# A decoder layer on one core: where fillers, low parts and broadcasts are placed

## The chip, the core and the metric

The kernel runs on one core of one Trainium2 chip. The metric is the device time of one execution in microseconds (us). Five engines run their own instruction queues beside each other: TensorE (PE, with its weight loads, PEld), VectorE (DVE), ScalarE (ACT), GpSimd (POOL), and SyncE (SP), which here only issues DMA transfers.

## The reference

One layer of a hybrid decoder: 1024 tokens, width 1024, all float32. An RMSNorm, one wide input projection, three token mixers on its columns (gated DeltaNet, mLSTM, sparse attention), each with its own projection and gates, a sum, an output projection, a SwiGLU network and a gated per-layer embedding. Cut to the parts that the change touches:

```python
# A: gated DeltaNet, 4 heads, chunks of 64 tokens
decay = jnp.where(tril, jnp.exp(jnp.where(tril, diff, 0.0)), 0.0)      # diff = gc_i - gc_j
X = jnp.where(strict, einsum('nbhid,nbhjd->nbhij', kb, kc) * decay, 0)
T = lax.linalg.triangular_solve(eye + X, eye, lower=True, unit_diagonal=True)
u, w = T @ (vc * bc), T @ (kb * jnp.exp(gc)[..., None])
# B: mLSTM, 4 heads: decay matrices of the same kind from i and f gates
# C: sparse attention, 8 heads in 2 groups, head width 64, 128 queries at a time
o = g_cmp * o_compressed + g_sel * o_selected + g_win * o_window       # gates from u
# merge, FFN
y = sum_b sigmoid(gate_b) * (out_b @ w_b);  h = x + y @ w_out
h = h + (silu(n(h) @ w1) * (n(h) @ w3)) @ w2
h = h + sigmoid(n(h) @ w_gate) * (p @ w_proj)                           # the per-layer embedding
```

## The kernel before, in words

**Precision.** Operands of the large products are kept as pairs of fp32r tiles: a high part (a rounded copy, made by ScalarE) and a low part (what is left, a subtraction). A product is three fp32r passes: high by high, high by low, low by high. `split` makes such a pair.

**Weights.** `run_blocks` streams the weights in blocks of four 128x512 tiles. SP loads `wraw` (four buffers), ACT casts `whi` (L429), and POOL, or for some tiles DVE, subtracts `wlo` (L431). The blocks' matmuls are named `mm`. After every third inner step a block yields, and `advance(rate)` then lets generators at the side issue a step or more each, so that their small matmuls and vector work are woven between the block's matmuls. A side generator can call `pause(us)`: it then yields until so much woven time, counted as 1.4 us per advance, has gone by. It so sets how many of the blocks' matmuls are issued ahead of the generator's next matmul, and, since SP's loads are issued with the blocks, the order on SP too. Nothing else sets the order: each engine runs its queue as issued.

**Stages.** From the start to about 874 us the input projection runs with the mixers' preparation at the side: `gates_side`, then four `gdn_solve`, four `mls_side`, then the attention's keys and compression, and beside these `gdn_scan`, the recurrence. From 874 to about 1311 us `nsa_attend` (attention) is woven with blocks of the merge gates at a rate of 3.8. From 1311 us on come the three branch projections, the output projection, the FFN (whose weight and activation products use sums of quarters, `ffn_combine` building four sums T1 to T4 and their high and low parts for each of eight rows of the model), and the per-layer embedding.

**The solve of a GDN head.** `gdn_solve` computes the gram matrices (`gram`), transposes keys (`ktr`), writes the diagonal blocks to DRAM and reads them back in another layout (`zds`, `zb`), solves them on DVE with 15 short steps, sends the inverses through DRAM (`xds`, then `zd`), spreads them by L908 into `gW` and `gV`, pauses 14.0, and then multiplies them up level by level (`levq`, `levv`, `levw`, ...). `row_bcast` makes a row of decays stand in all 128 partitions: POOL multiplies the identity by the column (L747, `gcb_d`), and a matmul with a matrix of ones sums it, in fp32.

**Attention.** A task is a branch (window or selected), a query tile and a pair of heads. `att_scores` makes four score rows `S`, DVE and ACT turn them into P, and P is scaled by the inverse sum, which has been multiplied by the gate (L1476), at L1478. `att_values` walks the key blocks of the task before: transposes P (`ptr`), copies the result to `PT` (DVE at L1570, ACT at L1572), and one block later multiplies the values (`nso`), two products of 64 output rows each, one per group, which stand in different halves of the array. After each of four quarters of the scores, a quarter of the values steps is issued. The compressed values `cv` are two products of 64 rows too.

Of the kernel before, what the change touches and what calls it, by code (L numbers as in the profile page):

```python
# [38 lines left out]
COMBINE_LAG = 8.0  # L39
CMP_AT = 1, 3  # L40
# [19 lines left out]
def _constants():  # L60
# [44 lines left out]
    add("rowscale", np.where((m >= 4) & (m < 8), -1.0, 1.0))  # L105
# [30 lines left out]
def _blocks(w_in, w_branch, w_out, w_ffn_in, w_ffn_out, w_ple_gate, w_ple_proj):  # L136
# [7 lines left out]
    for dst, src, n in ((0, 2048, 4), (4, 4108, 4), (8, 2052, 4), (12, 4104, 4), (16, 5392, 24)):  # L144
        rows[:, dst:dst + n] = w_in[:, src:src + n]
# [81 lines left out]
class Trunk:  # L227
# [381 lines left out]
    def gates_block(self):  # L609
# [4 lines left out]
        def evac(ct, hf, ps):  # L614
            if hf == 0:
                self.tc.keep_in_program_order(
                    nc.vector.tensor_tensor(bias, self.chan["rowb"], self.rowscale, OP.mult))
            nc.scalar.activation(rows[:40, hf * 512:hf * 512 + 512], ps[:40], AF.Identity,
                                 bias=bias[:40], scale=self.rowscale[:40])
            if hf == 1:  # L620
                self.flags.add("rows")

        self.gaterows = rows
        return self.chan_block(self.u, evac, ncols=1)

    def gates_side(self):
# [3 lines left out]
        ps = self.ps("gtr")  # L630
        for tt in range(NT):
            self.tr(ps[:, tt * 40:tt * 40 + 40], self.gaterows[:40, tt * P:tt * P + P])
        gm = self.b2("gm")[:, :320].rearrange("p (t c) -> p t c", c=40)
        nc.scalar.activation(gm, ps[:, :320].rearrange("p (t c) -> p t c", c=40), AF.Copy)
# [39 lines left out]
        self.cum, self.gcol = cum, gcol  # L674
# [62 lines left out]
        self.ms, self.msc, self.msi, self.memt, self.mwks, self.mr = s, sc, si, emt, wks, r  # L737
# [3 lines left out]
    def row_bcast(self, col, name):  # L741
# [3 lines left out]
        for hf in range(2):  # L745
            d = self.b2(name + "_d")
            nc.gpsimd.tensor_tensor(d[:, :].rearrange("p (t c) -> p t c", c=P), bc(self.ident.unsqueeze(1), [P, 4, P]),  # L747
                                    bc(col[:, 4 * hf:4 * hf + 4].unsqueeze(2), [P, 4, P]), OP.mult)
            ps = self.ps(name)
            self.mm(ps, self.ones, d)  # L750
            out.append(ps)
# [46 lines left out]
    def gdn_solve(self, h):  # L798
# [10 lines left out]
        dps = self.row_bcast(self.cum[:, :, h], "gcb")  # L809
# [20 lines left out]
        for w in H:  # L830
            for hf in H:
# [8 lines left out]
                yield from self.pause(1.4)  # L840
# [69 lines left out]
        yield from self.pause(14.0)  # L910
# [136 lines left out]
    def mls_side(self, h):  # L1047
# [6 lines left out]
        dps = self.row_bcast(self.mr[:, :, h], "mrb")  # L1054
# [188 lines left out]
    def nsa_keys(self, n, i):  # L1243
# [9 lines left out]
        for hf in range(2):  # L1253
# [10 lines left out]
            yield from self.pause(3.0)  # L1264
# [10 lines left out]
    def nsa_compress(self):  # L1275
# [3 lines left out]
        cv = self.small("cv", [P, 64])  # L1279
# [3 lines left out]
        for i, n in enumerate("kv"):  # L1283
# [13 lines left out]
            dst = ckr if n == "k" else cv  # L1297
# [9 lines left out]
            for g in range(2):  # L1307
                nc.vector.tensor_copy(dst[64 * g:64 * g + 63], ps[64 * g:64 * g + 63, :64])
# [28 lines left out]
        self.dump("cv", cv)  # L1337
# [10 lines left out]
    def nsa_attend(self):  # L1348
# [12 lines left out]
        for t in tasks + [None]:  # L1361
            a = self.att_scores(*t) if t else iter(())
# [698 lines left out]
```

## Time and profile before

| | |
|---|---|
| median of 3 runs | 2394.88 us (2393.13 to 2399.14) |
| the profiled execution's own time | 2392.93 us |
| its span, first to last instruction | 2391.1 us, mean granted clock 0.987 |
| busy: PE, PEld | 96%, 77% of the span |
| busy: DVE, ACT, POOL | 56%, 36%, 33% |
| DMA | 183 MB, mean 77 GB/s |

How to read the views: a row of waits reads "engine, its work, its line <- engine and work that released it: total us, times, longest us". A row of the timeline is "start, us, engine, line, work, operands, shape, count", with the idle time just before and what ended it in brackets; neighbours overlap, since matmuls are pipelined. A row of windows gives a stretch's length and then the busy time (and instruction count) of PE, PEld, DVE, ACT, POOL, the granted TensorE clock, the DMA share and GB/s. The chain of waits gives start, length and what ran. A row of groups gives count, total busy us, mean ns of one, and the idle time before it. Matmuls carry the line of a helper (L242, transposes L248 or L250).

### The profile page before, as it was taken

The numbers are of one execution on the slowest core, as the hardware profiler recorded it, in microseconds if no ns is written. First come the engines' busy times: TensorE is split into PE (matmuls) and PEld (weight loads), VectorE is DVE, ScalarE is ACT, GpSimd is POOL, SyncE is SP. The second block draws the span as 40 slices with busy tenths as digits, with TensorE's granted clock in tenths as the row PEclk, the third lists the DMA queues.
The fourth block names the chain that finished last, engine by engine and source line by source line (L and its number), as shares of the span: only waits on it lengthen the run. The fifth ranks groups of instructions, "written<-read, shape, count | busy, mean of one in ns | idle before, by whom it ended". The sixth has DMA issues, their size and how long they took to land.

```text
span 2391.1 us, 34586 instructions
## 1 busy us (share of the span) xinstructions
PE 2286.2 (96%) x12840; PEld 1829.4 (77%) x12840; DVE 1338.2 (56%) x3088; ACT 856.3 (36%) x1832; POOL 782.9 (33%) x662
## 2 busy tenths in 40 slices
PE   8989898989999998999999999998999999999999
PEld 6777677878778996666665778986777777777789
DVE  5455555643223436888775446677555555555583
ACT  6424242423222334545454322452222222222362
POOL 2342424322122123322121151235444444444434
PEclk9999999999999999999999999999999999999999
DMA  6131212121122123111111643311111111111143
GB/s 230 50 96 40 92 40 65 59 64 45 63 77 80 45 93 107 58 54 45 50 45 50 228 164 129 128 57 36 53 49 54 49 49 51 51 53 53 53 133 128
DMA packets 121887, 183.05 MB, mean 77 GB/s; under 512 B 25275, under 2 KB 47204, under 8 KB 121720
## 3 DMA queue, kind: packets, MB, share of 16 engines
q1 hardware_dynamic: 121432, 180.72, 22.5%
q8 instruction: 101, 1.65, 0.3%
q14 instruction: 66, 0.54, 0.1%
q10 hardware_dynamic: 288, 0.14, 0.0%
HBM read 149.04 MB, written 31.76 MB: 76 GB/s over the span
## 4 chain that ended last, share of the span: by engine, by line
PE 77%; DVE 12%; issue 4%; POOL 3%; DMA 3%; ACT 2%; SPq 0%; POOLq 0%; ACTq 0%; DVEq 0%
PE mm L242 60%; PE nso L242 3%; PE ptr L250 2%; PE S L242 2%; POOL wlo L431 2%; DVE P L1478 1%; DVE zb L893 1%; DVE xb L894 1%; PE mops L242 1%; PE gks L242 1%; PE gpu L242 1%; ACT g_junk L838 1%; POOL alo L1796 1%; ACT whi L429 1%; PE levq L242 1%
## 5 line engine op out<-in xcount | busy, mean ns | idle before, releaser
L431 POOL TENSOR_TENSOR wlo<-wraw,whi 128x512 fp32r<-128x512 f32 x334 | 449.7, 1351 | 1063.9 <-ACT whi L429 818.9
L242 PE MATMUL mm<-u,whi 128*128 128x512 f32 x1888 | 632.7, 410 | 2.0 <-ACT mg L1606 2.0
L429 ACT ACTIVATE whi<-wraw 128x512 fp32r<-128x512 f32 x408 | 255.7, 630 | 470.2 <-PE mm L242 384.0
L242 PEld LDWEIGHTS mm<-u,whi 128*128 128x128 f32 x1888 | 341.4, 190 | 76.0 <-issue 11.5
L242 PE MATMUL mm<-u,wlo 128*128 128x512 f32 x944 | 379.2, 402 | 0.0
L242 PEld LDWEIGHTS mm<-u,wlo 128*128 128x128 f32 x944 | 178.3, 189 | 39.4 <-issue 1.2
L1839 DVE TENSOR_TENSOR fc<-fc,mm 128x512 f32<-128x512 f32 x140 | 95.3, 686 | 159.0 <-PE mm L242 158.9
L1880 DVE TENSOR_TENSOR h<-h,mm 128x512 f32<-128x512 f32 x176 | 118.6, 684 | 74.6 <-PE mm L242 72.1
L242 PE MATMUL mm<-whi,alo 128*128 128x512 f32 x352 | 141.6, 402 | 6.8 <-POOL alo L1796 6.8
L242 PE MATMUL mm<-whi,ahi 128*128 128x512 f32 x352 | 140.7, 400 | 5.5 <-ACT whi L429 5.5
L242 PE MATMUL mm<-wlo,ahi 128*128 128x512 f32 x352 | 140.6, 399 | 2.5 <-POOL wlo L431 2.5
L431 POOL TENSOR_TENSOR wlo<-ws,whi 128x512 fp32r<-128x512 f32 x60 | 84.3, 1405 | 148.7 <-ACT whi L429 148.7
L242 PE MATMUL mm<-u2hi,whi 128*128 128x512 f32 x304 | 121.1, 398 | 0.0
L242 PE MATMUL mm<-u2lo,whi 128*128 128x512 f32 x304 | 121.1, 398 | 0.0
L242 PE MATMUL mm<-u2hi,wlo 128*128 128x512 f32 x304 | 120.3, 396 | 0.0
L1472 ACT ACTIVATE P<-P,n_ng 128x640 f32<-128x640 f32 (+7 forms) x128 | 93.0, 728 | 64.1 <-DVE n_ng L1470 61.1
L429 ACT ACTIVATE whi<-ws 128x512 fp32r<-128x512 f32 x60 | 37.8, 630 | 174.9 <-DVE h L1880 130.4
L250 PE MATMUL ptr<-ident,P 128*128 128x128 f32 x528 | 89.8, 282 | 7.3 <-DVE P L1478 5.5
L250 PEld LDWEIGHTS ptr<-ident,P 128*128 128x128 f32 x528 | 59.6, 140 | 47.2 <-issue 28.3
L242 PE MATMUL mm<-whi,u 128*128 128x256 f32 x512 | 94.1, 283 | 0.1
L431 DVE TENSOR_TENSOR wlo<-wraw,whi 128x512 fp32r<-128x512 f32 x74 | 69.5, 939 | 35.5 <-ACT whi L429 35.4
L242 PEld LDWEIGHTS mm<-whi,alo 128*128 128x128 f32 x352 | 66.8, 190 | 27.2 <-POOL alo L1796 11.6
(497 smaller groups left out, 5048.9 us busy)
## 6 DMA issues: line engine op xcount, KB each, us to landing
wraw<-in_w_dram SPq DMA_DIRECT2D x408, 256.0 KB, 2.7
mgs<-mg SPq DMA_DIRECT2D x48, 256.0 KB, 2.3
mgld<-mgs SPq DMA_DIRECT2D x48, 256.0 KB, 5.6
xt<-in_x_dram SPq DMA_DIRECT2D x8, 512.0 KB, 4.8
xt<-in_x_dram SPq DMA_DIRECT2D x32, 128.0 KB, 3.7
sg<-pps SPq DMA_DIRECT2D x32, 128.0 KB, 3.5
out_dram<-sg SPq DMA_DIRECT2D x32, 128.0 KB, 2.8
pps<-ppst SPq DMA_DIRECT2D x8, 256.0 KB, 2.0
```

Source lines behind the costliest of these rows:

```text
L242: return self.nc.tensor.matmul(out, lhsT, rhs, start=start, stop=stop).ins
L250: self.nc.tensor.transpose(out, in_, self.ident[:n, :n])
L429: nc.scalar.activation(hi, t, AF.Copy)
L431: eng.tensor_tensor(lo, t, hi.bitcast(F32), OP.subtract)
L838: nc.scalar.activation(junk, ps[:, q * P:q * P + P], AF.Square, accum_out=ssq[:, w, 4 * hf + q:4 * hf + q + 1])
L893: nc.vector.tensor_tensor(tmp[:, :m, m:], bc(Z[:, :m, m:m + 1], shp), bc(X[:, m:m + 1, m:], shp), OP.mult)
L894: nc.vector.tensor_tensor(X[:, :m, m:], X[:, :m, m:], tmp[:, :m, m:], OP.subtract)
L1472: nc.scalar.activation(pts[i][:, :nk], pts[i][:, :nk], AF.Exp, bias=ng[:, i:i + 1], accum_out=sm[:, g, i % 2:i % 2 + 1])
L1478: nc.vector.tensor_scalar(pts[i][:, :nk], pts[i][:, :nk], sm[:, g, i % 2:i % 2 + 1], None, OP.mult)
L1796: nc.gpsimd.tensor_tensor(lo, t, hi.bitcast(F32), OP.subtract)
L1839: nc.vector.tensor_tensor(t, x, ps, OP.add)
L1880: nc.vector.tensor_tensor(self.h[tt][s], self.h[tt][s], ps, OP.add)
```

## The change

1. **Gates block.** The 40 gate columns stand twice in a 128-column weight tile, at 0 and at 64. Four small DVE casts put their low parts at 64 to 103, in place of the second copy. Each half of the tokens then needs two passes of eight matmuls (weights by high, weights by low) rather than three; 104 rows are kept, `gates_side` transposes rows 0 to 39 and 64 to 103, and DVE adds the two.
2. **Decays.** `row_bcast` takes a column as a high and a low part (`col_split`), multiplies the identity by each on POOL, and sums them by two fp32r matmuls where one fp32 matmul stood. Four GDN heads (`gcb`) and four mLSTM heads (`mrb`) call it, each for two halves.
3. **Pauses.** 14.0 becomes 24.0 ahead of the levels of `gdn_solve`; 1.4 becomes 3.0 behind its second `ktr`; 3.0 becomes 6.0 in `nsa_keys` for the first half.
4. **Attention.** `att_values` transposes two key blocks in one step and multiplies the two of the step before; its steps are issued after the second, third and fourth quarter of the scores. The queries' preparation, `att_query`, is issued one task ahead. `cv` becomes block diagonal, one product of 128 rows. The gate (L1476) becomes the second scalar of the scaling of P.
5. **Low parts and sums from POOL to DVE.** The low parts of T1 to T4; the activations' low parts `alo` for the first two rows and every other half; the last sum of the embedding.
6. **Branch inputs.** For the second and third branch the split of each loaded tile is issued later, by 9.0 us and 2.56 us more per tile of matmul time, rather than at once.

The diff, cut to its core:

```diff
     for dst, src, n in ((0, 2048, 4), (4, 4108, 4), ...):
-        rows[:, dst:dst + n] = w_in[:, src:src + n]
+        rows[:, dst:dst + n] = rows[:, 64 + dst:64 + dst + n] = w_in[:, src:src + n]
...
+        def gen(wb):
+            for wh, wl in wb:
+                k2 = lambda t: t[:, :].rearrange("p (k c) -> p k c", k=2)[:, :, 64:104]
+                nc.vector.tensor_copy(k2(wh), k2(wl).bitcast(F32))
+            for hf in range(2):
+                ps = self.ps("mm", "mm")
+                for kc in range(KC):
+                    uh, ul = self.u(kc, hf)
+                    w = wb[kc // 2][0][:, kc % 2 * 256:kc % 2 * 256 + P]
+                    self.mm(ps, w, uh, kc == 0, False)
+                    self.last_mm = self.mm(ps, w, ul, False, kc == KC - 1)
...
+    def col_split(self, name, x):
+        hi, lo = self.small(name + "hi", list(x.shape), F32R), self.small(name + "lo", list(x.shape), F32R)
+        nc.vector.tensor_copy(hi, x)
+        nc.vector.tensor_tensor(lo, x, hi.bitcast(F32), OP.subtract)
+        return hi, lo
...
-            d = self.b2(name + "_d")
-            nc.gpsimd.tensor_tensor(d..., bc(self.ident...), bc(col[:, 4 * hf:4 * hf + 4]...), OP.mult)
             ps = self.ps(name)
-            self.mm(ps, self.ones, d)
+            for i, col in enumerate(cols):
+                d = self.b2(name + "_d", F32R)
+                nc.gpsimd.tensor_tensor(d..., bc(self.ident...), bc(col[:, 4 * hf:4 * hf + 4]...), OP.mult)
+                self.mm(ps, self.ones_r, d, i == 0, i == 1)
...
-                yield from self.pause(1.4)
+                yield from self.pause(3.0 if w else 1.4)
...
-        yield from self.pause(14.0)
+        yield from self.pause(24.0)
...
-            yield from self.pause(3.0)
+            yield from self.pause(6.0 if hf == 0 else 3.0)
...
-            nb = prev["nb"] + 2 if prev else 0
+            nb = -(-prev["nb"] // 2) + 2 if prev else 0
...
-                upto = -(-nb * (i + 1) // 4)
+                upto = -(-nb * i // 3)
...
+                if after and after[0] == "w" and after[2] == 0:
+                    if i == 0:
+                        ahead = self.att_query(after[1])
+                        next(ahead)
+                    elif i == 3:
+                        next(ahead)
...
-                nc.vector.tensor_tensor(sm[:, g], sm[:, g], gate[:, g], OP.mult)
                 for i in (n - 1, n):
-                    nc.vector.tensor_scalar(pts[i][:, :nk], pts[i][:, :nk], sm[:, g, i % 2:i % 2 + 1], None, OP.mult)
+                    nc.vector.tensor_scalar(pts[i][:, :nk], pts[i][:, :nk], sm[:, g, i % 2:i % 2 + 1],
+                                            gate[:, g, i % 2:i % 2 + 1], OP.mult, OP.mult)
...
-        for kb in range(nb + 1):
-            if kb < nb:
+        for kb in range(0, nb + 2, 2):
+            new = []
+            for b in range(kb, min(kb + 2, nb)):
                 ...
-            if pend is not None:
-                b, pt_ = pend
+                new.append((b, pt))
+            for b, pt_ in pend:
                 for g in range(2):
                     ...
-            pend = (kb, pt) if kb < nb else None
+            pend = new
             yield
...
-            for g in range(2):
-                gp = slice(64 * g, 64 * g + 64)
-                self.mm(o[gp, cols], st["cv"][gp], ct[gp, :256], False, hp == 1)
+            self.mm(o[:, cols], st["cv"].rearrange("p g d -> p (g d)"), ct[:, :256], False, hp == 1)
...
                 if first:
                     self.tc.keep_in_program_order(dma)
-                hi, lo = self.l2("yhi", F32R), self.l2("ylo", F32R)
-                self.split(hi, lo, t, scale)
-                res[kk, hf] = (hi, lo)
+                    parts(kk, hf, t)
+                else:
+                    self.later(Y_LAG + 2.56 * (4 * hf + kk), lambda kk=kk, hf=hf, t=t: parts(kk, hf, t))
...
-            nc.gpsimd.tensor_tensor(lo, t, hi.bitcast(F32), OP.subtract)     # part(), T1 to T4
+            nc.vector.tensor_tensor(lo, t, hi.bitcast(F32), OP.subtract)
...
-            nc.gpsimd.tensor_tensor(lo, t, hi.bitcast(F32), OP.subtract)     # put(), alo
+            (nc.vector if f < 2 or f % 2 and hf == 0 else nc.gpsimd).tensor_tensor(lo, t, hi.bitcast(F32), OP.subtract)
...
-                nc.gpsimd.tensor_tensor(t, t, h, OP.add)                     # the embedding's last sum
+                nc.vector.tensor_tensor(t, t, h, OP.add)
```

Where a pause is woven with blocks, the tables of instructions show the move. On SP, in the solve of the first head, before: the way of the solve's small blocks through DRAM (`zds`, `zb`, `xds`, `zd`) between weight loads (`wraw`) and stores of the merge gates (`mgs`).

```order
L882 DMA zds<-zd 128x8x16
L415 DMA wraw<-in_w_dram 128x512
L1608 DMA mgs<-mg 128x512
L884 DMA zb<-zds 64x256
L415 DMA wraw<-in_w_dram 128x512
L1608 DMA mgs<-mg 128x512
L415 DMA wraw<-in_w_dram 128x512 x3
L898 DMA xds<-xb 64x2x256
L1608 DMA mgs<-mg 128x512
L415 DMA wraw<-in_w_dram 128x512
L901 DMA zd<-xds 128x8x16 x2
```

The same place on SP with the change:

```order
L920 DMA zds<-zd 128x8x16
L1656 DMA mgs<-mg 128x512
L922 DMA zb<-zds 64x256
L416 DMA wraw<-in_w_dram 128x512 x3
L1656 DMA mgs<-mg 128x512
L416 DMA wraw<-in_w_dram 128x512
L936 DMA xds<-xb 64x2x256
L1656 DMA mgs<-mg 128x512
L939 DMA zd<-xds 128x8x16 x2
```

The order of the four transfers is kept, one store still stands between `xds` and the two reads of `zd`, and no weight load stands there now. On PE the rows `mm` of 128x512 between a head's last gram and its first `levq` number 89, 89, 90 and 90 in the four heads before, and 132 in each with the change. The last rows of the first stage's side work (`ncmp`, `nctr`, `khtr`) stand 16 `mm` earlier in PE's order, which is what the gates block has lost.

On PE in the attention, at a window task (`nvw` are its values), before:

```order
L242 MATMUL mm<-u,whi 128x512
L242 MATMUL nso<-PT,nvw 64x256 x2
L250 MATMUL ptr<-ident,P 128x128 x4
L242 MATMUL nso<-PT,nvw 64x256 x2
L242 MATMUL S<-khh,qT 128x256
L242 MATMUL S<-kll,qT 128x256
L242 MATMUL mm<-u,whi 128x512
L242 MATMUL nso<-PT,nvw 64x256 x2
L250 MATMUL ptr<-ident,P 128x128 x4
```

With the change, at the like place:

```order
L243 MATMUL mm<-u,whi 128x512
L251 MATMUL ptr<-ident,P 128x128 x4
L243 MATMUL nso<-PT,nvw 64x256 x6
L243 MATMUL S<-khh,qT 128x256
L243 MATMUL S<-kll,qT 128x256
L251 MATMUL ptr<-ident,P 128x128 x4
L243 MATMUL S<-khh,qT 128x256
L243 MATMUL S<-kll,qT 128x256
```

In the whole program the 132 pairs of `nso` over window and selected blocks (one product of 64 rows for each group) stand in 126 unbroken runs before and in 85 with the change, where 14 pairs are split by other work between their two products. Of the blocks' `mm` 469 stand between the first `S` and the last `nso` before, and 380 with the change.

On DVE in `ffn_combine` (`uw` builds the sums T1 to T4, `sil` is the FFN's gate product), before:

```order
L1769 TENSOR_TENSOR uw<-u2hi,u2lo 128x512 x3
L1805 TENSOR_TENSOR sil<-sil,mm 128x512
L1774 TENSOR_TENSOR uw<-uw 128x512
L1776 TENSOR_TENSOR uw<-uw 128x512
L1778 TENSOR_TENSOR uw<-uw 128x512
L1769 TENSOR_TENSOR uw<-u2hi,u2lo 128x512
L1781 TENSOR_TENSOR uw<-uw 128x512
L1805 TENSOR_TENSOR sil<-sil,mm 128x512
```

With the change:

```order
L1825 TENSOR_TENSOR uw<-u2hi,u2lo 128x512 x3
L1830 TENSOR_TENSOR uw<-uw 128x512
L1832 TENSOR_TENSOR uw<-uw 128x512
L1820 TENSOR_TENSOR utT1l<-uw,utT1h 128x512
L1834 TENSOR_TENSOR uw<-uw 128x512
L1820 TENSOR_TENSOR utT3l<-uw,utT3h 128x512
L1825 TENSOR_TENSOR uw<-u2hi,u2lo 128x512
L1820 TENSOR_TENSOR utT2l<-uw,utT2h 128x512
L1837 TENSOR_TENSOR uw<-uw 128x512
L1862 TENSOR_TENSOR sil<-sil,mm 128x512
L1820 TENSOR_TENSOR utT4l<-uw,utT4h 128x512
L1853 TENSOR_TENSOR alo<-sil,ahi 128x512 x2
```

The four subtractions that make the low parts, and the first two `alo`, now stand in DVE's queue between the sums, where POOL ran them before.

More of the change, by code (lines that the diff above doesn't have):

```diff
@@ L39 @@
 COMBINE_LAG = 8.0
+Y_LAG = 9.0
 CMP_AT = 1, 3
@@ L617, in evac @@
                     nc.vector.tensor_tensor(bias, self.chan["rowb"], self.rowscale, OP.mult))
[L618 to L619 removed]
+            nc.scalar.activation(rows[:104, hf * 512:hf * 512 + 512], ps[:104], AF.Identity,
+                                 bias=bias[:104], scale=self.rowscale[:104])
             if hf == 1:
                 self.flags.add("rows")
+        def gen(wb):
[9 more added lines that the diff above has]
+                    self.last_mm = self.mm(ps, w, ul, False, kc == KC - 1)
+                    if kc % 3 == 2:
+                        yield
+                evac(0, hf, ps)
+                self.passed(KC * 0.43)
+                yield
         self.gaterows = rows
[L624 removed]
+        return gen
     def gates_side(self):
@@ L629, in gates_side @@
         yield from self.need("rows")
-        ps = self.ps("gtr")
-        for tt in range(NT):
-            self.tr(ps[:, tt * 40:tt * 40 + 40], self.gaterows[:40, tt * P:tt * P + P])
         gm = self.b2("gm")[:, :320].rearrange("p (t c) -> p t c", c=40)
-        nc.scalar.activation(gm, ps[:, :320].rearrange("p (t c) -> p t c", c=40), AF.Copy)
+        for r in (0, 64):
+            ps = self.ps("gtr")
+            for tt in range(NT):
+                self.nc.tensor.transpose(ps[:, tt * 40:tt * 40 + 40], self.gaterows[r:r + 40, tt * P:tt * P + P],
+                                         self.ident[r:r + 40, r:r + 40])
+            p3 = ps[:, :320].rearrange("p (t c) -> p t c", c=40)
+            if r == 0:
+                nc.scalar.activation(gm, p3, AF.Copy)
+            else:
+                nc.vector.tensor_tensor(gm, gm, p3, OP.add)
         yield
@@ L673, in gates_side @@
         nc.scalar.activation(ekd, p8[:, 4, :, 0:4], AF.Exp)
-        self.cum, self.gcol = cum, gcol
+        self.cumhl, self.gcol = self.col_split("cum", cum[:, :, 0:4]), gcol
+        self.ones_r = sm("ones_r", [P, P], F32R)
+        nc.vector.tensor_copy(self.ones_r, self.ones)
         yield
@@ L807, in gdn_solve @@
         half = lambda ap, hf: ap[:, hf * 512:hf * 512 + 512]
-        dps = self.row_bcast(self.cum[:, :, h], "gcb")
+        dps = self.row_bcast([c[:, :, h] for c in self.cumhl], "gcb")
         yield
@@ L1053, in mls_side @@
         yield from self.need("mls_gates", ("m", h, "k"))
-        dps = self.row_bcast(self.mr[:, :, h], "mrb")
+        dps = self.row_bcast([c[:, :, h] for c in self.mrhl], "mrb")
         yield
@@ L1307, in nsa_compress @@
             for g in range(2):
-                nc.vector.tensor_copy(dst[64 * g:64 * g + 63], ps[64 * g:64 * g + 63, :64])
+                rows = slice(64 * g, 64 * g + 63)
+                nc.vector.tensor_copy(ckr[rows] if n == "k" else cv[rows, g], ps[rows, :64])
             yield
@@ L1360, in nsa_attend @@
         prev = None
-        for t in tasks + [None]:
+        for _ in self.att_query(0):
+            pass
+        for n, t in enumerate(tasks + [None]):
             a = self.att_scores(*t) if t else iter(())
+            after = (tasks + [None] * 2)[n + 1]
             b = self.att_values(prev) if prev else iter(())
             cur = None
-            nb = prev["nb"] + 2 if prev else 0
+            nb = -(-prev["nb"] // 2) + 2 if prev else 0
             done = 0
@@ L1397, in att_query @@
             out.append(t)
-        return out
+        yield
     def att_scores(self, br, qt, hp):
@@ L1614, in load_y, with parts @@
         res = {}
+        def parts(kk, hf, t):
+            hi, lo = self.l2("yhi", F32R), self.l2("ylo", F32R)
+            self.split(hi, lo, t, scale)
+            res[kk, hf] = (hi, lo)
         for hf in range(2):
```

28 lines of the change are left out of this document (15 added, 13 removed).

## The prediction

> **What bounds the kernel now.** I read the page's busy shares first, then what TensorE (PE) waited for, then the stretches in which it waited.
>
> ```profile
> PE 2286.2 (96%) x12840; PEld 1829.4 (77%) x12840; DVE 1338.2 (56%) x3088; ACT 856.3 (36%) x1832; POOL 782.9 (33%) x662
> ```
>
> PE is the bound: 2391.1 − 2286.2 = 104.9 us of the span are idle, and everything else must come from work removed from PE or from a slower clock. The waits say what ended the idle time:
>
> ```profile
> PE levq L242 <- DVE gW L908: 30.0, 4, 8.5
> PE mm L242 <- POOL alo L1796: 6.8, 11, 1.7
> PE mm L242 <- POOL wlo L431: 6.2, 7, 2.5
> PE qtr L248 <- DVE qstk L1388: 6.2, 8, 1.7
> PE mm L242 <- ACT whi L429: 5.5, 1, 5.5
> PE ptr L250 <- DVE P L1478: 5.5, 12, 0.8
> PE khtr L248 <- ACT khht L1261: 3.2, 2, 1.7
> PE ktr L250 <- ACT g_junk L838: 3.0, 3, 1.3
> PE nso L242 <- DVE PT L1570: 3.0, 3, 1.5
> ```
>
> These nine make 69.4 of the 104.9 us, and the change aims at each of them. The first is four waits, one per GDN head. What it costs beyond the idle time is in the stretches:
>
> ```profile
> 160.00:170.00 10.00, 10.00 (x164) 8.00 (x162) 2.67 (x4) 1.22 (x2) 2.54 (x2) 0.78 0.11 34
> 960.00:1020.00 60.00, 56.24 (x306) 37.42 (x306) 50.87 (x199) 33.17 (x82) 17.90 (x18) 1.00 0.20 67
> 1020.00:1080.00 60.00, 56.73 (x324) 36.74 (x324) 52.79 (x199) 31.40 (x73) 15.86 (x16) 1.00 0.14 49
> 1630.00:1640.00 10.00, 6.11 (x16) 4.51 (x17) 7.16 (x8) 4.49 (x8) 10.00 (x7) 0.55 0.17 57
> ```
>
> After PE stood still the granted clock falls (0.78 in 160 to 170, 0.55 in 1630 to 1640), so such a wait costs its length and some us more. In the attention (the rows of 60 us) the clock is 1.00, PE is busy 56 to 57 of 60 and VectorE (DVE) already 51 to 53.
>
> **1. The pause ahead of levq: −37.**
>
> ```profile
> 158.25 1.27 DVE L908 TENSOR_TENSOR gW<-zd,c 128x512 f32<-128x512 f32 x1 [6.14 <-DMA zd<-xds]
> 159.67 1.97 PE L242 MATMUL levq<-gW,zak 64*64 64x64 f32 x32 [7.85 <-DVE gW L908]
> 167.05 1.15 PE L242 MATMUL levq<-gW,zak 64*64 64x64 f32 x32
> 1699.24 57.75 PE mm L242 x246
> ```
>
> PE waits 7.85 us for `gW`, which itself waited for the inverse to come back through DRAM. The chain's row of 246 `mm` in 57.75 us gives 0.235 us for one. The order puts 132 rather than 89 or 90 of them between the last gram and levq, 43 × 0.235 = 10.1 us of work, against 7.5 us of idle per head (30.0 / 4; the longest is 8.5). That leaves 1.6 to 2.6 us if `gW` is not later. I take it not to be: on SyncE the order of the four transfers is kept, with one store between `xds` and `zd` as before. The first levq took 1.97 us where the warm one took 1.15, and the `mm` around it run slow too; a clock of 0.78 over 10 us is 2.2 us lost, of which I count 1.7 per head, 7 in all. So −30 − 7 = −37. If `gW` comes 3 us later, 1 us per head stays and some of the slow clock: −26. No work is removed here, so the fillers must come from elsewhere. They are taken from the blocks behind, which go on to the mLSTM and attention preparation; in the order, the last items at the side stand where they stood in the stream of `mm`, 16 rows earlier, which is what the gates block lost. So the pause doesn't push work past the stage's end.
>
> **2. ktr and khtr: −4.3** of the 6.2 us in their two rows, by 1.6 and 3.0 more of woven time against longest waits of 1.3 and 1.7; −2 to −6.2.
>
> **3. Gates block: −3.1.** 16 matmuls fewer, 16 × 0.235 = 3.8; eight more transposes, which by the row below are 0.9 busy and about 0.7 on the path. DVE's four casts and one addition lie beside PE, which has the next block. −2 to −3.8.
>
> ```profile
> L250 PE MATMUL gtr<-ident,gaterows 40*128 40x40 f32 x8 | 0.9, 235 | 0.0
> 177.21 1.72 PE gcb L242 x4
> 173.14 1.04 POOL L747 TENSOR_TENSOR gcb_d<-ident,cum 128x512 f32<-128x512 f32 x1
> ```
>
> **4. Broadcasts: −6.2.** The two fp32 matmuls of a head are four records and 1.72 us on the chain; four fp32r ones are 4 × 0.235 = 0.94. Eight calls: 8 × 0.78 = 6.2. POOL does 16 more products of 1.04 us. It is busy 33% of the span, and I take them as hidden, with 1 us put into term 10; if nothing hid them, +16.
>
> **5. Attention, products: −9.**
>
> ```profile
> 961.63 0.65 PE L242 MATMUL nso<-PT,nvs 128*64 128x256 f32 x4
> 962.22 0.65 PE L242 MATMUL nso<-PT,cv 64*64 64x256 f32 x4
> 962.80 0.73 PE L242 MATMUL mm<-u,whi 128*128 128x512 f32 x2
> 1083.01 1.08 PE L242 MATMUL nso<-PT,nvw 128*64 128x256 f32 x8 [1.47 <-DVE PT L1570]
> 1084.02 0.66 PE L250 MATMUL ptr<-ident,P 128*128 128x128 f32 x4
> ```
>
> A pair of half-array products (four records) holds PE from 961.63 to 962.22, 0.59 us; two pairs from 1083.01 to 1084.02, 1.01 us. So a pair is 1.01 − 0.59 = 0.42 and leaving a run costs 0.17; entering costs something too, which no row isolates, and I estimate 0.1. Runs fall from 126 to 85: 41 × 0.28 = 11.5 saved. 14 pairs are broken, and I let each product then take 0.42 alone, 14 × 0.42 = 5.9 lost: −5.5. `cv` is 0.58 from 962.22 to 962.80; one product of 128 rows by 256 columns in fp32 is half of a 128x512 (1.72 / 2 = 0.86), 0.43, and it enters no other mode: 16 × 0.22 = −3.5. The ends: no gain from fewer runs and broken pairs at full price +6 less `cv`, +2; broken pairs free −16.
>
> **6. Attention, waits: −9.** The rows `qtr`, `ptr` and `nso` are 14.7 us. The query, one task ahead, should take its 6.2 whole. The rest waits for DVE, which loses the 64 gate products,
>
> ```profile
> L1476 DVE TENSOR_TENSOR n_sum<-n_sum,cgate 128x2 f32<-128x2 f32 x64 | 19.4, 304 | 0.7
> ```
>
> 19.4 us, but now finds its values in three quarters of a task rather than four. I take a third of the remaining 8.5: −9, from 0 to −15.
>
> **7. FFN sums: −11.**
>
> ```profile
> 1592.32 0.68 DVE L1776 TENSOR_TENSOR uw<-uw 128x512 f32<-128x512 f32 x1
> 1593.04 1.70 DVE L1778 TENSOR_TENSOR uw<-uw 128x512 f32<-128x512 f32 x1
> 1592.89 1.30 POOL L1764 TENSOR_TENSOR utT1l<-uw,utT1h 128x512 fp32r<-128x512 f32 x1 [17.80 <-ACT utT1h L1763]
> 1625.40 0.50 PE L242 MATMUL mm<-whi,alo 128*128 128x512 f32 x1 [1.72 <-POOL alo L1796]
> 1631.37 0.79 PE L242 MATMUL mm<-whi,ahi 128*128 128x512 f32 x1 [5.48 <-ACT whi L429]
> 1634.68 0.79 PE L242 MATMUL mm<-wlo,ahi 128*128 128x512 f32 x1 [2.52 <-POOL wlo L431]
> ```
>
> The same DVE subtraction took 0.68 us alone and 1.70 when POOL ran beside it, and POOL's own took 1.30 to 1.76. So each low part on POOL slowed both. On DVE alone a set of T1 to T4 with its low parts and two `alo` is 12 operations of about 0.65, 8 us, within the 8.0 us of matmul time that the kernel's lag sets between two of them, though with nothing to spare. POOL is then free for `wlo`, and the three waits, 9.7 us with 2 more of slow clock behind (0.55 in 1630 to 1640), should go nearly whole: −11. If DVE falls behind at that rate half comes back: −5.
>
> **8. alo in the later rows: −4.7.**
>
> ```profile
> 1822.07 0.63 ACT L1795 ACTIVATE ahi<-fc 128x512 fp32r<-128x512 f32 x1 [1.95 <-DVE fc L1857]
> 1822.78 1.28 POOL L1796 TENSOR_TENSOR alo<-fc,ahi 128x512 fp32r<-128x512 f32 x1 [1.29 <-ACT ahi L1795]
> 1824.12 0.51 PE L242 MATMUL mm<-whi,alo 128*128 128x512 f32 x1 [0.52 <-POOL alo L1796]
> ```
>
> About 0.5 us ten times (6.8 less the 1.7 already counted): a DVE subtraction of 0.68 ends 0.6 sooner than POOL's 1.28. −4.7, from 0 to −5.1.
>
> **9. Tail and branch inputs: −4.** Near the end POOL does two sums between weights' low parts, and PE waits for the second:
>
> ```profile
> 2315.71 2.06 POOL sg L1967 x2
> 2317.78 1.68 POOL wlo L431
> 2319.50 2.54 PE mm L242 x19
> 1348.95 0.50 PE L242 MATMUL mm<-yhi,whi 128*128 128x512 f32 x1 [1.24 <-DVE acc L1658]
> ```
>
> 2.06 of POOL go, so PE starts up to 1.8 sooner; the branch loads' splits no longer stand before `acc`, 1.24 and a like one; and a little at the very end. −1 to −4.5.
>
> **10. New waits: +6.** Nothing in the trace shows them. A stretch with fewer fillers behind the solve, attention with 380 `mm` rather than 469, the POOL products: 0 to +25, the upper end being the attention's waits once over (14.7) and, for the first stage, one head's wait for `gW` and those before khtr (7.5 + 3.2). I take the lower part, since PE's idle time outside the named waits is only 104.9 − 69.4 = 35.5 us in the whole program.
>
> **The sum.** −37 − 4.3 − 3.1 − 6.2 − 9 − 9 − 11 − 4.7 − 4 + 6 = −82.3. On the profiled execution's 2392.93 that is 2310.6; the median of the runs is 1.95 above the profiled one, so 2312.6, and I say 2312.
>
> **Rivals.**
>
> *The pause only moves the wait.* If the return through DRAM is tied to the blocks' loads, `gW` comes later with the pause, and about half of term 1 stays: 2312 + 19 = 2331. For it: `gW` waited for the transfer, not for DVE. Against: the order of the queue.
>
> *Attention becomes VectorE's.* DVE is at 51 to 53 of 60 us. With 89 fewer `mm` as cover (21 us of PE work, moved into the time after it), DVE has to do its work in less time. If its busy share can't pass 90%, terms 5 and 6 give nothing and some 5 us come on top: 2312 + 18 + 5 = 2335. Against: 19.4 us of its work go.
>
> *No new waits at all, and every term near its far end:* 2312 − 6 − 16 = 2290.
>
> [...]
>
> [...]
>
> **How the numbers follow.** Forecast 0.57, the pause rival 0.12, DVE 0.16, all lands 0.12, half clock 0.03. The likeliest's own range is 2290 to 2330. With the DVE rival and a little over it the range is 2288 to 2345, and what lies outside is part of the all-lands case and the half clock, and misses of several terms at once. A change within 0.3% (7 us, about what a measurement of this kernel tells from none) needs 75 us of the sum to fail: 0.02. Slower is the half clock at its price: 0.03. Faster 0.95.
>
> **What would show it.** Idle before levq under 1 us and the clock at 1.00 in the 20 us after; `nso` runs of eight records or more, at 0.42 per pair; no `qtr` wait; DVE below 55 of 60 in the attention; no wait over 1 us between 1620 and 1640's counterpart; `gcb` at 0.94. The forecast is wrong if PE's waits on DVE in the attention exceed 15 us, if the time before levq merely shifts to `gW` again, or if the granted clock falls there.

## The result, and the profile after

The change takes 2328.11 us (median; 2327.02 to 2329.65), against 2394.01 us for the kernel before on the same chip: a ratio of 0.9721, 95% interval [0.9704, 0.9738]. The forecast was 2312, the range 2288 to 2345. So 66 us were gained where 82 were expected; the study asks where the other 16 went. The profiled execution took 2327.02 us, its span is 2325.2.

The page's busy times of the change:

```profile
PE 2263.7 (97%) x12800; PEld 1836.2 (79%) x12800; DVE 1332.0 (57%) x3096; ACT 852.3 (37%) x1832; POOL 729.1 (31%) x616
```

PE's idle time fell from 104.9 to 61.5 us, its busy time by 22.5 us. The waits on PE in the change (the longest groups, others left out):

```profile
PE ptr L251 <- DVE P L1525: 7.5, 12, 1.1
PE gytr L251 <- DVE vtok L1050: 5.4, 2, 3.1
PE warm L251 <- DMA ident<-in_c_dram: 5.0, 1, 5.0
PE u2tr L251 <- DVE u2lo L321: 4.7, 3, 2.0
...
PE mm L243 <- POOL wlo L432: 4.1, 5, 3.1
PE mtr L251 <- DVE m_tmp L737: 2.9, 1, 2.9
...
PE mm L243 <- ACT utT4h L1819: 2.0, 1, 2.0
PE gpu L243 <- DVE gvn L1025: 1.9, 3, 0.9
...
PE gks L243 <- DVE gS L1032: 1.5, 2, 1.0
PE khtr L249 <- ACT khht L1299: 1.5, 2, 0.8
```

The rows before levq, qtr and for `alo` are gone. In their place stand `gytr` (the transposes at the end of a GDN head's recurrence), a wait of 3.1 us for `wlo`, and a longer one for `m_tmp` (ahead of `mtr`, a transpose among the mLSTM gates), none of which the kernel before had at this size. `gpu` and `gks` are small products of the recurrence. The first levq in the timeline of the change, and stretches around it, around gytr and in the attention (windows):

```profile
171.45 1.15 PE L243 MATMUL levq<-gW,zak 64*64 64x64 f32 x32
```

```profile
160.00:170.00 10.00, 6.92 (x24) 5.41 (x24) 1.43 (x1) 0.60 (x1) 3.96 (x3) 0.83 0.51 142
170.00:180.00 10.00, 10.00 (x180) 7.88 (x179) 2.67 (x4) 0.60 (x1) 1.05 (x1) 1.00 0.01 2
228.00:238.00 10.00, 6.91 (x30) 5.37 (x29) 5.92 (x10) 4.09 (x20) 2.44 (x3) 0.83 0.36 132
926.00:986.00 60.00, 56.58 (x311) 39.80 (x312) 52.07 (x202) 33.84 (x84) 19.35 (x19) 0.97 0.17 58
986.00:1046.00 60.00, 57.72 (x351) 41.24 (x346) 51.91 (x205) 34.32 (x78) 13.62 (x13) 1.00 0.14 49
```

levq no longer waits and is warm (1.15 us), but just ahead of it, in 160 to 170, PE is busy for only 6.92 of 10 us, and again around gytr.

By stages, from the first start of a stage's first matmul in the two timelines: up to the first `S` the change is 33.7 us earlier (921.3 to 887.6); from there to the first branch product it gains another 12.7 (to 1333.6 and 1287.2, both including the 89 `mm` that moved behind the attention); to the first product with `ahi` 1.5; to the last one 15.2; to the end 2.8. So the FFN gave what was forecast, the attention a third less, and the first stage 33.7 where the terms 1 to 4 made 50.6.

The two traces let a stage be split further, into PE's idle time, what slow clock cost (by an estimate half of PE's busy time wherever the clock record stands at a half: from one `mm` to the next it is 0.427 us there in the median, and 0.231 at full clock, in both traces), and the rest, which is PE's work. Up to the first `S` idle time fell from 53.9 to 33.7 us, the cost of slow clock from 14.1 to 8.5, and the work from 853.3 to 845.5. From there to the first branch product idle time fell from 19.0 to 12.2, slow clock went from none to 1.7, and the work fell from 393.2 to 385.7. Stages are used below where the whole time, in which stretches of half clock come and go from one execution to the next (the mean granted clock was 0.992 to 0.994 in the four runs of the change), is too coarse; each is read from one profiled execution of a kernel.

### The profile page after: what moved, and what is told of

Same layout as the page of the kernel before. It is cut to its first block, busy times and chain, and to the rows that moved or that the text cites. A ratio compares the mean times of both kernels' runs of the same rounds, so it can differ in the third digit from the quotient of the medians.

```text
span 2325.2 us, 34431 instructions
## 1 busy us (share of the span) xinstructions
PE 2263.7 (97%) x12800; PEld 1836.2 (79%) x12800; DVE 1332.0 (57%) x3096; ACT 852.3 (37%) x1832; POOL 729.1 (31%) x616
## 4 chain that ended last, share of the span: by engine, by line
PE 84%; DVE 10%; issue 2%; ACT 2%; DMA 1%; POOL 1%; SPq 0%; ACTq 0%; POOLq 0%; DVEq 0%
PE mm L243 68%; PE nso L243 3%; PE ptr L251 2%; PE S L243 2%; DVE P L1525 1%; PE mops L243 1%; PE gks L243 1%; PE gram L243 1%; PE gpu L243 1%; DVE P L1514 1%; POOL wlo L432 0%; DVE uw L1825 0%; DVE kT L824 0%; DVE xn L1778 0%; PE u2tr L251 0%
## 5 line engine op out<-in xcount | busy, mean ns | idle before, releaser
L432 POOL TENSOR_TENSOR wlo<-wraw,whi 128x512 fp32r<-128x512 f32 x334 | 443.8, 1335 | 1021.8 <-ACT whi L430 790.0
L243 PE MATMUL mm<-u,wlo 128*128 128x512 f32 x928 | 374.2, 403 | 3.1 <-POOL wlo L432 3.1
L432 DVE TENSOR_TENSOR wlo<-wraw,whi 128x512 fp32r<-128x512 f32 x74 | 64.5, 871 | 46.0 <-ACT whi L430 46.0
```

Of the source, the lines that this page charges most:

```text
L243: return self.nc.tensor.matmul(out, lhsT, rhs, start=start, stop=stop).ins
L432: eng.tensor_tensor(lo, t, hi.bitcast(F32), OP.subtract)
```

## The experiments

All times are medians of the run; ratios are to the kernel before on the same chip, and "the change" is the 2328.11 us (0.9721) above.

**The pause, in the change and alone.**

```diff
-        yield from self.pause(24.0)      # in the change
+        yield from self.pause(14.0)
```

> The change with the pause ahead of levq back at 14.0; all other parts stay. Theory A (the terms of the forecast add up, the pause is worth 37 us): 2328 + 37 = 2365 us, with the four waits of 7 to 8 us before levq back. Theory B (the pause removes those waits whole, some 40 us with the slow clock behind them, but takes the fillers that covered the end of the recurrence, gytr, and a weight's low part on POOL, whose waits of 5.4 and 3.1 us with the slow clock behind them are then its price): 2328 + 22 to 28 = 2350 to 2356 us, the waits before gytr and the one of 3.1 us for wlo gone. Between the last gpu and gytr stand 50, 37, 19 and 42 mm here, against 24, 23, 23 and 31 in the change.

2339.31 us, 0.9767 [0.9751, 0.9783]: the pause is worth 11 us in the change, less than either theory gave (15.5 by its stage: the first `S` comes at 903.1 rather than 887.6 us). One row of its waits:

```profile
PE levq L243 <- DVE gW L946: 20.9, 4, 8.3
```

They were 20.9 us and not 30.0: two heads waited 7.2 and 8.3, the other two 3.1 and 2.3. There the time from the start of the last gram to levq is 24 to 25 us, against 28 to 30 in the first two heads and in all four before, though 85 to 90 `mm` stand between in all of them. Something on the way to `gW` had become faster without being edited.

The same edit alone, on the kernel before:

```diff
-        yield from self.pause(14.0)      # in the kernel before
+        yield from self.pause(24.0)
```

> The kernel before with the one edit 14.0 to 24.0 ahead of levq. Theory A: 2394 - 37 = 2357 us. Theory B: 13, 18, 32 and 37 mm stand between the last gpu and gytr (42, 42, 18, 48 before), at 0.235 us 3.1 and 4.2 us against a chain on DVE of some 8 us: waits of 4 to 5 us at gytr in the first two heads, each with about 2 us of slow clock, and 3 + 2 us for wlo: 2394 - 40 + 13 + 5 = 2372 us, at least 2365.

2364.34 us, 0.9871 [0.9856, 0.9886]: −31 alone, between the theories. PE waits at gytr for 0.3 us at most, though in the first two heads only 13 and 18 `mm` stand ahead of it, against 24 and 23 in the change; the waits for `wlo` rose from 6.2 to 11.9 us. The count of fillers alone does not make the wait at gytr.

**The cause at gytr.** The timelines of the change around its longest wait, PE, then POOL, then DVE's chain that ends in `vtok`:

```profile
231.43 1.27 PE L251 MATMUL gytr<-ident,vtok 128*128 128x128 f32 x8 [3.09 <-DVE vtok L1050]
```

```profile
224.66 1.29 POOL L432 TENSOR_TENSOR wlo<-wraw,whi 128x512 fp32r<-128x512 f32 x1 [1.27 <-ACT whi L430]
226.23 1.32 POOL L432 TENSOR_TENSOR wlo<-wraw,whi 128x512 fp32r<-128x512 f32 x1 [0.28 <-ACT whi L430]
227.81 2.53 POOL L432 TENSOR_TENSOR wlo<-wraw,whi 128x512 fp32r<-128x512 f32 x2 [0.26 <-ACT whi L430]
```

```profile
224.47 0.17 DVE L296 TENSOR_TENSOR rsq_tgo<-rsq_ygo 128x8 f32<-128x8 f32 x1
224.67 1.31 DVE L297 SCALAR_TENSOR_TENSOR rsq_tgo<-rsq_tgo,g_s 128x8 f32<-128x8 f32 x1
226.02 0.17 DVE L298 SCALAR_TENSOR_TENSOR rsq_ygo<-rsq_tgo,rsq_ygo 128x8 f32<-128x8 f32 x1
...
226.42 1.16 DVE L297 SCALAR_TENSOR_TENSOR rsq_tgo<-rsq_tgo,g_s 128x8 f32<-128x8 f32 x1
...
228.01 1.13 DVE L297 SCALAR_TENSOR_TENSOR rsq_tgo<-rsq_tgo,g_s 128x8 f32<-128x8 f32 x1
229.17 1.19 DVE L298 SCALAR_TENSOR_TENSOR rsq_ygo<-rsq_tgo,rsq_ygo 128x8 f32<-128x8 f32 x1
```

Four operations of eight elements a row take 1.13 to 1.31 us where their like take 0.17, each while POOL works on a `wlo`, and each ends 0.024 to 0.030 us after that `wlo` does: here one small operation was held until POOL's instruction ended. Together the four are 4.1 us longer than four of 0.17, and PE's wait is 3.09. That can be tried.

```diff
-                self.run_blocks(blocks, 2, 0, self.setup2)   # first stage: no wlo on DVE
+                self.run_blocks(blocks, 2, 2, self.setup2)   # 140 of its 145 wlo on DVE
```

> The change with all low parts of the weights of the first stage (wlo) made by DVE, none by POOL. Theory (DVE's small operations that take 1.1 to 1.3 us where their like take 0.17 are held up by POOL's wlo of 1.3 us, and that made the waits for gytr): in the recurrence's end all rows of 128x8 at 0.17 to 0.2 us, no wait over 0.5 us before gytr, none for wlo on POOL; 2328 - 10 = 2318 us if DVE bears the load. Rival 1 (the 1.1 us are the operations' own, or the engine's): the same rows of 1.1 us stay. Rival 2 (some 0.65 us for each low part, about 45% of DVE's time being taken already, make DVE late elsewhere): over 2328 us, though the rows of 128x8 are short.

2309.68 us, 0.9642 [0.9622, 0.9663]: 19 us faster than the change (by the ratios), where the theory had 10. Of these, 15.7 lie ahead of the first `S`, which comes at 871.9 rather than 887.6 us. The rows of the same tile in the change and with this edit (count; least, median and longest ns):

```profile
L297 DVE SCALAR_TENSOR_TENSOR rsq_tgo<-rsq_tgo,g_s x12: 166/168/1315, 224.7 to 574.0; 128x8 f32<-128x8 f32 x12
```

```profile
L297 DVE SCALAR_TENSOR_TENSOR rsq_tgo<-rsq_tgo,g_s x12: 159/166/168, 219.9 to 560.9; 128x8 f32<-128x8 f32 x12
```

The longest falls from 1315 to 168 ns, and the waits at gytr and for `wlo` on POOL are all but gone (0.2 and 0.3 us). DVE bore the load: a `wlo` takes it 0.69 us (0.686 in the median of the 74 that it makes in the change). The stall has the size of one instruction of POOL: the longest row is 1.315 us, a `wlo` on POOL 1.295 in the median. What makes the one wait for the other was not shown.

**The same edit on the kernel before** asks whether the 30 us before levq were made the same way.

> The kernel before with the one edit that DVE makes the weights' low parts of the first stage; the pause stays 14.0. Theory (the wait before levq itself was made longer by POOL's wlo holding up the solve's small operations on DVE): from the last gram to gW 24 to 26 us in each head rather than 29 to 30, as in the two heads of the change with pause 14.0 whose small operations ran beside no wlo; 97 to 99 mm stand there now (89 or 90 before), 23 us; so 1 to 3 us of wait per head instead of 7.5, and little slow clock: 2394 - 24 - 6 = 2364 us, 2358 to 2372. Rival (the chain through the DRAM sets the wait, not DVE): gram to gW stays at 29 us, 2394 - 8 (mm more) = 2385 us or more.

2352.77 us, 0.9827 [0.9813, 0.9842]: −41 us by this one edit, a time below the theory's range, and more than the longer pause gave alone. The waits at levq, then the solve's small steps (L894) before and with the edit:

```profile
PE levq L242 <- DVE gW L908: 6.8, 4, 1.9
```

```profile
L894 DVE TENSOR_TENSOR xb<-xb,zb x60: 165/208/1329, 140.9 to 494.9; 64x15 f32<-64x15 f32 x8, 64x28 f32<-64x28 f32 x8, 64x39 f32<-64x39 f32 x8, 64x48 f32<-64x48 f32 x8
```

```profile
L894 DVE TENSOR_TENSOR xb<-xb,zb x60: 166/200/218, 140.4 to 466.6; 64x15 f32<-64x15 f32 x8, 64x28 f32<-64x28 f32 x8, 64x39 f32<-64x39 f32 x8, 64x48 f32<-64x48 f32 x8
```

From the start of the last gram to levq it now takes 25.3 to 26.0 us in all heads, 3.1 to 4.7 less than before. These are 14.9 of the 23.2 us by which the waits fell; the rest is near the 8.5 us of the 36 `mm` more that stand there (97 to 99 a head, 0.235 us each). So the wait that the pause covers was in good part POOL's doing.

**The new waits taken away by fillers instead.**

```diff
-        for eng, M, w in ((nc.gpsimd, V, 0), (nc.vector, W, 1)):
+        for eng, M, w in ((nc.vector, V, 0), (nc.vector, W, 1)):
...
-        yield from self.pause(8.0)       # ahead of gytr
+        yield from self.pause(14.0)
```

> The change with two edits against the new waits of its first stage: gV is spread by DVE, so that no low part of a weight stands on POOL behind an operation that waits for the DRAM, and the pause ahead of gytr is 14.0 rather than 8.0 (47 to 73 mm in place of 23 to 31 between the last gpu and gytr). Theory (these waits of 5.4 and 3.1 us and the half clock for 3 to 4 us behind each are what the forecast had not counted): 2328 - 12 = 2316 us, 2314 to 2320. Rival (fillers taken for one wait are missed at the next): 2325 to 2330 us, with new waits of the same size elsewhere in the first stage.

2312.65 us, 0.9659 [0.9641, 0.9677], 15 us faster than the change, 3 beyond the theory's value; up to the first `S`, which now comes at 876.1 us, it is 11.5, close to the theory's 12. No gytr row is left, and none of the waits for `wlo` on POOL in the first stage is above 0.3 us. In the change `gV` had waited on POOL for the transfer `zd`, with two `wlo` queued behind it:

```profile
160.87 1.04 POOL L946 TENSOR_TENSOR gV<-zd,c 128x512 f32<-128x512 f32 x1 [6.30 <-DMA zd<-xds]
161.86 2.96 POOL L432 TENSOR_TENSOR wlo<-wraw,whi 128x512 fp32r<-128x512 f32 x2
```

**The decays' broadcast.** In place of two fp32r passes one fp32 matmul again, and one product on POOL per half.

```diff
-            for i, col in enumerate(cols):
-                ...
-                self.mm(ps, self.ones_r, d, i == 0, i == 1)
+            nc.gpsimd.tensor_tensor(d..., bc(self.ident...), bc(cols[:, 4 * hf:4 * hf + 4]...), OP.mult)
+            self.mm(ps, self.ones, d)
```

> The change with the decays broadcast by one fp32 matmul per half again, and one product on POOL for it rather than two. Forecast (term 4): eight calls at 1.72 rather than about 0.97 us, 2328 + 6 = 2334 us. Rival (the 16 further products on POOL, 1.04 us each, hold up weights' low parts and small operations of DVE, so that the edit is worth nothing or costs): 2322 to 2329 us.

2327.96 us, 0.9723 [0.9703, 0.9743]: no difference, where 6 us were expected; an effect of up to some 5 us can't be told apart by this. The stages tell it apart. Up to the first `S`, which all eight calls precede, this kernel takes 894.7 us, the change 887.6, and four other kernels here with the change's first stage 885.7 to 888.7. Of the 7.1 us, 4.8 are PE's work (850.3 against 845.5). Behind that point, where the edit changes nothing, its profiled execution is 3.7 us shorter, mostly since it lacks two stretches of half clock that the change's has. So the term holds in its stage. The work fell in the change's timeline, where from the call's start to the next matmul it is 1.01 us rather than 1.72:

```profile
187.19 1.18 PE L243 MATMUL gcb<-gcb_d,ones_r 128*128 128x512 f32 x4
188.20 0.62 PE L243 MATMUL mm<-u,whi 128*128 128x512 f32 x2
```

One counterweight shows: the wait before the second `mtr`, in the change and with the fp32 broadcast.

```profile
74.83 0.22 PE L251 MATMUL mtr<-ident,m_crow 32*128 32x32 f32 x1 [2.86 <-DVE m_tmp L737]
```

```profile
75.05 0.21 PE L251 MATMUL mtr<-ident,m_crow 32*128 32x32 f32 x1 [1.04 <-DVE m_crow L719]
```

It is 1.8 us longer in the change, and 3.4 us of half clock follow it, which cost 1.7, so a part of the 8 × 0.7 = 5.6 us that the broadcasts save may be paid back here. Other waits are longer with the fp32 broadcast, though, and the idle time up to the first `S` is 34.8 us there against 33.7. That POOL's further products lengthen the wait before `mtr` was not tried by itself.

**The attention.** First the values one block at a time, in four quarters (the rest of the attention's edits stay):

```diff
-            nb = -(-prev["nb"] // 2) + 2 if prev else 0
+            nb = prev["nb"] + 2 if prev else 0
...
-                upto = -(-nb * i // 3)
+                upto = -(-nb * (i + 1) // 4)
...
-        for kb in range(0, nb + 2, 2):
+        for kb in range(0, nb + 1, 1):             # and min(kb + 1, nb) below
```

> The change with values taken one block at a time again and issued in four quarters; the block-diagonal cv, the folded gate and the query ahead stay. If merging runs of nso is worth what the forecast put on it (5.5 us, and a part of the waits of the attention): 2328 + 5 to 8 = 2333 to 2336 us. Rival (runs cost little to enter and leave, and the waits of ptr for P, 7.5 us in the change against 5.5 before, come from issuing values in three quarters): 2325 to 2329 us.

2331.15 us, 0.9730 [0.9714, 0.9745]: 2 to 3 us, below the 5 to 8 of the forecast and hardly clear of the rival. The stage says more. From the first `S` to the first branch product it takes 406.6 us here and 399.6 in the change (398.5 to 399.9 in six other kernels with the change's attention): 7.0 us, of which 4.2 are PE's work (389.9 against 385.7) and 2.9 its waits (15.1 against 12.2), with one stretch of half clock in each. So merging the runs is worth what was forecast. The whole times show less of it: the mean granted clock was 0.992 to 0.994 in the runs of the change and 0.994 or 0.995 in these, which by an estimate (the means differ by 0.0017, of 2330 us) is worth 4 us. Then the query in its own task:

```diff
+            for _ in self.att_query(qt):           # at the head of att_scores; the calls one task ahead removed
+                pass
```

> The change with the queries prepared at the start of their own task again. Forecast (in term 6): the waits of qtr for qstk, 6 us in eight places, come back: 2328 + 6 = 2334 us, 2332 to 2338. Rival (the waits go to ptr for P, 7.5 us in the change, wherever DVE does the query's work): 2326 to 2330 us.

2356.75 us, 0.9846 [0.9824, 0.9868]: 29 us slower than the change, where 6 were expected. Its waits in the attention:

```profile
PE qtr L249 <- DVE qstk L1428: 13.4, 8, 3.4
PE qtr L249 <- DVE n_top L1582: 3.6, 1, 3.6
...
PE ptr L251 <- DVE pc L1545: 2.9, 5, 1.7
```

17 us at qtr, and seven stretches of half clock in the attention where the change has one. Then both together:

> The change with both the query in its own task and values one block at a time in four quarters (the two edits undone that were undone singly: the query alone gave 2356.8 us, the values alone 2331.2). If the two add: 2328 + 28.6 + 3 = 2360 us. Theory (the late, paired issue of the values is what makes a query in place so dear: its DVE copies stand ahead of the query's work in DVE's queue; with values in quarters only the 6 us of before come back): 2331 + 6 to 8 = 2337 to 2340 us, and the waits of qtr near 6 us.

2333.05 us, 0.9752 [0.9736, 0.9769]: some 5 to 7 us above the change, 24 below the query alone, and below the theory's 2337 to 2340. The waits for the query are small again:

```profile
PE qtr L249 <- DVE qstk L1428: 5.4, 6, 1.6
```

The two edits do not add. With paired values issued late, a query in place costs 29 us; with values in quarters 2 to 5, hardly clear of noise. By the attention's stage it is 31.0 us (430.6 against 399.6) and next to nothing (406.5 against 406.6). The look-ahead mostly pays for what the pairing brought, and both together are worth 5 to 7 us. That DVE's copies of the late values stand ahead of the query's work is the theory's reason for it, and was not tried by itself.

**The FFN's low parts** of T1 to T4 and all `alo` on POOL again:

```diff
-            nc.vector.tensor_tensor(lo, t, hi.bitcast(F32), OP.subtract)     # part()
+            nc.gpsimd.tensor_tensor(lo, t, hi.bitcast(F32), OP.subtract)
...
-            (nc.vector if f < 2 or f % 2 and hf == 0 else nc.gpsimd).tensor_tensor(lo, ...)
+            nc.gpsimd.tensor_tensor(lo, ...)
```

> The change with the low parts of T1 to T4 and all alo back on POOL. Forecast (terms 7 and 8, which the span from the first to the last alo product, 15.2 us shorter than before, seems to bear out): 2328 + 15 = 2343 us. Rival (most of these 15 us came from other edits, as the later splits of the branch inputs): under 2335 us.

2342.60 us, 0.9782 [0.9764, 0.9799]: 14.5 us, as forecast, and the three rows of before are back (waits from 1500 us on):

```profile
PE mm L243 <- POOL alo L1853: 6.5, 11, 1.7
PE mm L243 <- ACT whi L430: 5.5, 1, 5.5
PE mm L243 <- POOL wlo L432: 2.5, 1, 2.5
```

**A faster version.** The change, with the first stage's `wlo` on DVE, 14.0 ahead of gytr, and 7.0 rather than 2.0 ahead of the second mtr:

> The change with the low parts of the first stage's weights on DVE, the pause ahead of gytr 14.0, and the pause behind the running maximum of the mLSTM gates (ahead of the second mtr) 7.0 rather than 2.0 (23 mm in place of 6). If the gains of the first two were one and the same cause met in two ways, and the wait of 2.9 us for m_tmp with 3 us of half clock goes: 2310 - 5 = 2305 us. If they add: 2295 us.

2303.78 us, 0.9622 [0.9607, 0.9636]: the nearer value. With `wlo` on DVE alone the wait before the second `mtr` was 2.9 us and the slow clock there cost 3.3, which is all of the 5.9 us gained on that run. The fillers ahead of gytr added nothing, so the two edits met one cause. Then the same with the attention's `wlo` on DVE too:

```diff
-                self.run_blocks([self.mg_block(b, 1) for b in range(MG_ATT)], ATT_RATE)
+                self.run_blocks([self.mg_block(b, 1) for b in range(MG_ATT)], ATT_RATE, 2)
```

> The kernel of the label b1 (2303.8 us) with the weights' low parts of the attention on DVE as well. Theory (POOL's operation of 1.3 us costs DVE more beside it than the 0.68 us that DVE takes for it): the 13 us of waits of the attention on DVE and ACT fall by half, 2304 - 6 = 2298 us. Rival (DVE, at 50 to 53 us busy of 60 in the attention, has no room): 2304 to 2315 us, with more waits of ptr for P.

2295.99 us, 0.9586 [0.9572, 0.9600], 32 us below the change. One of its windows in the attention and the row for P:

```profile
986.00:1046.00 60.00, 58.72 (x351) 42.16 (x350) 53.21 (x192) 33.14 (x75) 5.33 (x7) 1.00 0.18 62
```

```profile
PE ptr L251 <- DVE P L1525: 3.5, 8, 1.0
```

The window does not hold the same work as the one of the change, since the attention starts 23 us earlier here. Over the whole attention, from the first `S` to the last `nso`, DVE is busy for 85.7% of the time rather than 83.0, and PE's waits fall from 11.2 to 7.9 us (the theory had half). The 32 `wlo` that took POOL 42.4 us take DVE 22.1, but DVE's busy time rises by 7.0 alone (294.4 to 301.4). So by an estimate (22.1 − 7.0) some 15 us of its busy time had been stalls beside POOL, and 52 of 60 did not mean that there was no room.

## Why the prediction was right or wrong

**Term 1, the pause (−37): mechanism right, worth mis-sized.** All four waits at levq went, as forecast, and levq ran warm. With the 30.0 us went 9.8 us of slow clock behind them, where the prediction counted 7, so the removal itself was not too small. But in the company of the other edits only 20.9 of the 30.0 us were left to be covered, and the net of the pause was 11 us. The step that failed is "the fillers must come from elsewhere", which was followed only to the end of the stage and not to the next generator that waits: gytr (5.4 us in two waits) and `wlo` behind `gV` (3.1 us), with half clock behind each of the three. The prediction quoted the row that shows the cause, DVE's subtraction of 1.70 beside POOL, but used it for the FFN alone.

**Term 10, new waits (+6): too small.** The first stage's new rows are 5.4 for gytr, 3.1 for `wlo`, 1.8 more for mtr, and some 3 for gpu and gks: 13 us, and four episodes of half clock of 1.7 each, 7 us: 20 in all. Against the 6 of the sum that is 14 of the 16 us that were missed. Taking away gytr's waits and `wlo`'s gave 2312.65, within 1 us of the forecast, but that close an agreement is partly luck: the attention still lacks 5 us of its terms, and stretches of half clock come and go.

**Terms 2 and 3** came out: ktr's row is gone and khtr fell from 3.2 to 1.5, −4.7; `gtr` starts 2.6 us and ends 3.1 us earlier. **Term 4** (−6.2): the work fell by 0.7 a call, and the first stage, by the run above, by 5 to 7 us; the whole time does not show it.

**Terms 5 and 6 (−18): 12.7.** PE's work in the attention's stage fell by 7.5 us and its waits by 6.8, where 9 were forecast for each, and one stretch of half clock came in, 1.7. Of the work, merging the runs gave 4.2 (5.5 forecast). The price per pair held:

```profile
946.77 1.56 PE L243 MATMUL nso<-PT,nvw 128*64 128x256 f32 x12
948.25 0.39 PE L243 MATMUL S<-khh,qT 128*128 128x256 f32 x1
```

Three pairs take 1.48 us, 0.44 each after 0.17 for the run. The 0.1 for entering a run, which the prediction took from no row, is in the trace before: from an `mm` to the start of the `nso` behind it is 0.327 us in the median, to another `mm` 0.234. The broken pairs may have taken what is missing; no run shows their price. The other 3.3 us of work are those that one block at a time leaves in place, near the 3.5 forecast for `cv`; no run undid `cv` by itself. Of the waits, ptr for P rose from 5.5 to 7.5, but it is 6.9 with values in quarters too. The look-ahead was filed as a wait of 6.2 us removed; its real part was to make the pairing bearable.

**Terms 7 to 9 (−19.7): 19.5** by the stages above, and 14.5 by undoing 7 and 8, for which 15.7 stood. One sign of the prediction failed here: at the counterpart of 1631 us, 1582.94 in the change, PE still waits 2.04 us, now for `utT4h` on ACT, with a stretch of half clock behind it.

**The rivals.** That the pause only moves the wait gave 2331, near the measured time, but by a mechanism that is not there: `gW` ends 24.2 to 30.3 us after the start of the last gram in the change, and 28.6 to 30.1 before. The wait moved to other generators. VectorE as the attention's bound is refuted by the last kernel, which gives DVE more work there and is faster. Half clock through the attention, to which the prediction gave 0.03, did not come: the clock was 0.97 and 1.00 in the two windows above. There was one episode of 3.4 us in it, behind two waits for P of 0.9 us with one `ptr` between them and three after. Nor did transposes alone keep the clock down at the start of the traces, where 48 `warm` transposes, made by the same helper as `ptr`, run from 4.99 us on with nothing else on PE:

```profile
L251 PE MATMUL warm<-ident x48: 272/421/476, 5.0 to 12.8; 128*128 128x128 f32 x48
```

They follow each other at 0.213 us up to 10.4 us and at 0.109 from 10.7 on, and the record of full clock begins at 10.5. So transposes by themselves released the clock here.

One sentence of the section on the kernel was too strong: the order is not set by the pauses alone, since the same 8.0 ahead of gytr stood for 42 `mm` before and 24 in the change, in the first head.

## What to carry to other kernels

When fillers are moved to cover a wait, count them at every later wait that lived on them, and ask first why the awaited chain is slow: its rows' least and longest durations (0.166 and 1.315 us for `rsq_tgo`) show a stall that the mean hides. Small dependent VectorE operations beside a stream of GpSimd work took 1.13 to 1.31 us here where their like took 0.17; moving the stream to VectorE, which looked the busier engine, was worth 41 us in the kernel before, by one argument of a call. Two edits that share an engine's queue have to be tried together and apart, as the query and the pairs show. And a small edit is judged by the length of its stage, with idle time and slow clock split off, where the whole time moves by as much from one execution to the next.

## What the hardware showed beyond expectation

In these traces the price of a wait on PE has a step. Over the 14 profiles of this study (those before and after, and the twelve runs), waits of 0.5 us and more that stood alone (no other within 6 us, the start left out) were followed by a stretch at half clock in 4 of 276 cases where they lasted under 1.9 us, in 31 of 65 from 1.9 to 2.6 us, and in 28 of 31 above. (Many of these are the same wait in several kernels, so they are fewer independent cases than the counts say.) One stretch lasts 3.41 us in the clock record and costs 1.7, by the estimate above the half of it; some are two or three times as long (6.83 and 10.24 us before) and cost 2 to 4. The same wait of 1.95 us before `u2tr` (transposes ahead of the FFN) was followed by it in the change and not with pause 14. So by an estimate the last half microsecond of a wait of 2 us can be worth four times its length (0.5 us of wait and 1.7 of slow clock).
